# A Fourier token mixer: half of one projection moves from fp32 products to three fp32r passes, under a new table of side steps

## The chip, the core and the metric

The kernel runs on one core of one Trainium2 chip. The metric is the device time of one execution in microseconds (us): 186.82 before, the median of three runs (186.81 to 186.85). TensorE (PE) multiplies and loads its stationary weights (PEld), VectorE (DVE), ScalarE (ACT) and GpSimd (POOL) do the elementwise work, and SyncE (SP) issues most of the transfers. Each engine works through its own instructions in program order and waits on semaphores for the others.

## The reference, cut to what matters

With a depth of one, only the Fourier layer runs. It works on 512 latent tokens and, as a sequence of its own, 128 context tokens, with a width of 1024:

```python
def fourier_mix(u):                      # 4 groups of 256 channels
    ug = u.reshape(b, s, 4, 256)
    return real(fft2(ug, axes=(1, 3), norm="ortho"))   # over positions and channels

def fourier_layer(x, cond, norm_w, w_mod, b_mod, w_in, w_out):
    shift, scale, gate = split(silu(cond) @ w_mod + b_mod, 3)
    h = rms_norm(x, norm_w) * (1 + scale) + shift
    u, z = split(h @ w_in, 2)
    y = fourier_mix(u) * silu(z)
    return x + gate * (y @ w_out)
```

The outputs are the layer's result for both sequences; the two others stay empty. The results have to be close to float32.

## The kernel before

All 640 tokens are in flight together. The weights are cut into 48 pieces of 128 rows by 512 columns, and the program is a walk over 48 units n, one for each piece:

- n = 0 to 15 make z, n = 16 to 31 make u (16 to 23 the first two groups, 24 to 31 the last two), n = 32 to 47 multiply by w_out.
- Where fp32 accuracy is wanted from the faster fp32r type, an operand is split into a high half (a cast on ScalarE, `high_piece`) and a low half (the difference, mostly on VectorE, `low_piece`), and three products are added: high by high, high by low, low by high. `three` gives these pairs, and z and w_out are made so.
- u is made differently. The transform over positions is applied to the normalised input before the product with the weights (`sequence`, f16 in two halves, L575), since the product commutes with it. The input is first folded over the symmetry of the cosine and sine tables: `fold_first` to `fold_sin` make five parts c, co, so, se, ce for each quarter q of 256 channels, and `fold_split` makes f16 halves of them. `evacuate` writes the result for input chunk k, scaled by (1 + scale), as x_k. Then `product_u` (L616) multiplies x_k with the weight piece in one fp32 product per f (four to a piece, in halves of 324 and 318 columns). One fp32 product is two instructions in the profile. `fold_piece` (L210, L211) first replaces a piece's two halves by their sum and difference, which is the first step of the channel transform, and asks for piece n + 5.
- `channel` (L691 to L706) is the channel transform, in fp32r three passes, `channel_out`, `channel_last` and `alternate` assemble y, `scale_z` multiplies z by the rms factor row `rb`, `silu_z` applies SiLU, `mix` multiplies and `split_y` halves y for w_out.
- The rms factors r256 (one column per 128 tokens) are wanted along the free axis too. `spread_rms` writes them to DRAM (`rms_row`), reads them back spread over all partitions (`rt`), and `order_rms` copies them on POOL into the order of the bins.
- The conditioning: `modulate` (L296) makes the scale for chunk k on TensorE, `weigh` (L313) makes shifts and gates by a weighted sum on VectorE, one row of 1024 per condition and 128 outputs.

What runs beside the products is tied to positions in that walk: `at(n, i, step)` puts a step ahead of product i of unit n, and `run(n, i)` issues what is put there. The first eight units have their side steps written between the products (`go_ahead`, `weigh_part`). The place in the walk sets the order on every engine, and a step's transfers come into SP's queue there, too: `load_piece` waits for the buffer that its piece is to fill, and everything behind it in the queue waits with it.

Of the kernel before, what the change touches and what calls it, by code (L numbers as in the profile page):

```python
# [35 lines left out]
EVEN = np.concatenate([4 * np.arange(1, 64), 4 * np.arange(64) + 2, [0, 256]])  # L36
# [18 lines left out]
C_SEL, C_KV, C_FIRST, C_LOW, C_MISC = 0, 2, 4, 6, 7  # L55

# [56 lines left out]
def fourier_step(ctx: ExitStack, tc: tile.TileContext, a):  # L113
# [84 lines left out]

    nc.scalar.dma_start(small, a["small"])
# [34 lines left out]
    idle = const.tile([P, 512], F16, name="idle")  # L234
# [223 lines left out]
    def silu_z(e):  # L458
        for j, cols in ((1, slice(0, SL)), (0, slice(SL, T))):
            z = zs[:, e, cols]  # L460
            nc.scalar.activation(z, z, AF.Silu, bias=zs[:, e, T + j : T + j + 1])
# [6 lines left out]
    def open_folds():  # L468
# [3 lines left out]
        for n in ("ce", "se", "co", "so", "c"):  # L472
            fold[n] = [p.tile([P, D], F16, name=f"{n}_{q}") for q in "hl"]
# [10 lines left out]
    def spread_rms():  # L484

        row = dram.tile([1, 5 * P], F32, name="rms_row")
        nc.sync.dma_start(row.rearrange("o (j p) -> (o p) j", p=P), r256)
        pools["rt"] = tmp.tile([P, SL], F32, name="rt", tag="turn")
        for out, cols in ((pools["rt"], slice(0, SL)), (rb[:, SL:T], slice(SL, T))):
            nc.sync.dma_start(out, row[:, cols].to_broadcast(out.shape))  # L490

    def order_rms():
        rt = pools.pop("rt")
        for at, src in (
            (0, rt[:, 1:128:2]), (64, rt[:, 255:128:-2]),
            (128, rt[:, 4:129:4]), (160, rt[:, 252:128:-4]), (191, rt[:, 2:128:4]), (223, rt[:, 254:128:-4]),
            (255, rt[:, 0:257:256]), (257, rt[:, 385:512:2]), (321, rt[:, 383:256:-2]),
            (385, rt[:, 388:512:4]), (416, rt[:, 384:256:-4]), (448, rt[:, 386:512:4]), (480, rt[:, 382:256:-4]),
        ):
            nc.gpsimd.tensor_copy(rb[:, at : at + src.shape[-1]], src)  # L500


    fold, part = {}, {}
# [4 lines left out]
    class Parts(dict):  # L508
# [5 lines left out]
        def __missing__(self, n):  # L514
            self[n] = pools["fold"].tile([P, 256], F32, name=f"{n}_{self.q}", tag=n, bufs=1)
# [11 lines left out]
    def fold_context(q):  # L527
        c = parts_of(q)["c"] = xn[4][:, columns(q)]
        nc.scalar.activation(c, c, AF.Identity, scale=r256[:, 4:5])
# [20 lines left out]
    def fold_split(q, *names):  # L550
        for n in names:
            x = part[q][n]
# [595 lines left out]
```

## Time and profile before

| | |
|---|---|
| median of three runs | 186.82 us |
| the profiled execution | 186.77 us |
| its span | 185.0 us |
| PE busy | 179.8 us (97%), 1137 instructions |
| DVE busy | 144.5 us (78%), 318 |
| ACT busy | 88.6 us (48%), 201 |
| POOL busy | 17.5 us (9%), 57 |
| granted TensorE clock | 1.00 |

The span is the profiler's time from the first to the last instruction; 1.8 us of the execution's time lie outside it. In the views, a line names a place in the kernel printed above, `out<-in` are the program's names for the tiles, and "idle before" is how long the engine stood ahead of an instruction, with what released it. A busy engine is not the same as a limiting one: an engine counts where its work ends last.

### The profile page before, as it was taken

The numbers are of one execution on the slowest core, as the hardware profiler recorded it, in microseconds if no ns is written. First come the engines' busy times: TensorE is split into PE (matmuls) and PEld (weight loads), VectorE is DVE, ScalarE is ACT, GpSimd is POOL, SyncE is SP. The second block draws the span as 40 slices with busy tenths as digits, with TensorE's granted clock in tenths as the row PEclk, the third lists the DMA queues.
The fourth block names the chain that finished last, engine by engine and source line by source line (L and its number), as shares of the span: only waits on it lengthen the run. The fifth ranks groups of instructions, "written<-read, shape, count | busy, mean of one in ns | idle before, by whom it ended". The sixth has DMA issues, their size and how long they took to land.

```text
span 185.0 us, 3209 instructions
## 1 busy us (share of the span) xinstructions
PE 179.8 (97%) x1137; PEld 146.4 (79%) x1137; DVE 144.5 (78%) x318; ACT 88.6 (48%) x201; POOL 17.5 (9%) x57
## 2 busy tenths in 40 slices
PE   7999999999999998999999999999999999999993
PEld 2677777789999978877685786768878889999992
DVE  0444468998999999799998795589869969999422
ACT  3353733359950066977436546778774035210000
POOL 3000000000061005600002031020210000000000
PEclk9999999999999999999999999999999999999999
DMA  5999999999944007843168243120421453703532
GB/s 185 378 408 405 402 404 406 395 390 405 333 152 114 0 4 191 261 190 115 53 230 320 69 113 115 36 78 0 117 58 57 170 182 132 245 12 148 210 131 82
DMA packets 15648, 35.58 MB, mean 192 GB/s; under 512 B 2448, under 2 KB 3472, under 8 KB 15504
## 3 DMA queue, kind: packets, MB, share of 16 engines
q1 hardware_dynamic: 15488, 35.33, 53.7%
q8 instruction: 9, 0.15, 0.4%
q10 hardware_dynamic: 144, 0.04, 0.1%
q14 instruction: 7, 0.06, 0.1%
HBM read 32.75 MB, written 2.62 MB: 191 GB/s over the span
## 4 chain that ended last, share of the span: by engine, by line
PE 76%; DVE 13%; ACT 6%; DMA 2%; issue 1%; DVEq 0%
PE acc L369 25%; PE acc L616 14%; PE h L406 8%; PE s L406 8%; PE acc L379 6%; DVE junk L313 5%; PE pl L575 3%; PE pm L296 3%; DVE wl L225 3%; PE spare L280 2%; DMA ws<-in_w_in 2%; ACT zs L453 1%; PE pc L575 1%; PE acc L624 1%; ACT wh L218 1%
## 5 line engine op out<-in xcount | busy, mean ns | idle before, releaser
L616 PE MATMUL acc<-x,folded 128*128 128x324 f32 (+1 forms) x128 | 36.9, 438 | 0.0
L616 PEld LDWEIGHTS acc<-x,folded 128*128 128x128 f32 x128 | 23.5, 190 | 9.6 <-issue 1.0
L225 DVE TENSOR_TENSOR wl<-ws,wh 128x512 fp32r<-128x512 f32 x27 | 18.0, 687 | 3.0 <-ACT wh L218 2.8
L218 ACT CAST wh<-ws 128x512 fp32r<-128x512 f32 x27 | 16.3, 617 | 7.6 <-PE h L406 7.5
L313 DVE SCALAR_TENSOR_TENSOR junk<-wg,cb 128x1024 bf16<-128x1024 f32 x16 | 19.5, 1222 | 0.3
L307 DVE TENSOR_SCALAR a<-pm,b_scale,nw 128x2 f32<-128x2 f32 x8 | 2.2, 279 | 15.2 <-PE pm L306 15.1
L369 PE MATMUL acc<-yh,wh 128*128 128x512 f32 x32 | 13.0, 408 | 0.1
L369 PE MATMUL acc<-yl,wh 128*128 128x512 f32 x32 | 12.6, 394 | 0.0
L369 PE MATMUL acc<-yh,wl 128*128 128x512 f32 x32 | 12.6, 393 | 0.0
L340 ACT ACTIVATE hh<-xt,a 128x128 fp32r<-128x128 f32 (+1 forms) x15 | 7.5, 546 | 9.4 <-DVE a L307 9.4
L406 PE MATMUL h<-hl,wh 128*128 128x256 f32 (+1 forms) x40 | 11.0, 292 | 0.0
L406 PE MATMUL h<-hh,wh 128*128 128x256 f32 (+1 forms) x40 | 11.0, 292 | 0.0
L406 PE MATMUL h<-hh,wl 128*128 128x256 f32 (+1 forms) x40 | 11.0, 292 | 0.0
L406 PE MATMUL h<-yh,wh 128*128 128x256 f32 (+1 forms) x40 | 11.0, 292 | 0.0
L406 PE MATMUL h<-yl,wh 128*128 128x256 f32 (+1 forms) x40 | 11.0, 291 | 0.0
L406 PE MATMUL h<-yh,wl 128*128 128x256 f32 (+1 forms) x40 | 11.0, 290 | 0.0
L369 PE MATMUL acc<-hh,wl 128*128 128x512 f32 x32 | 10.9, 417 | 0.0
L313 DVE SCALAR_TENSOR_TENSOR junk<-folded,cb 128x1024 bf16<-128x1024 f32 x8 | 9.8, 1221 | 0.1
L313 DVE SCALAR_TENSOR_TENSOR junk<-wr,cb 128x1024 bf16<-128x1024 f32 x8 | 9.8, 1220 | 0.1
L369 PE MATMUL acc<-hh,wh 128*128 128x512 f32 x32 | 9.4, 416 | 0.1
L369 PE MATMUL acc<-hl,wh 128*128 128x512 f32 x32 | 9.3, 396 | 0.0
L347 DVE SCALAR_TENSOR_TENSOR hl<-xt,a,hh 128x512 fp32r<-128x512 f32 (+1 forms) x16 | 8.1, 548 | 1.2 <-ACT hh L340 1.2
(210 smaller groups left out, 456.1 us busy)
## 6 DMA issues: line engine op xcount, KB each, us to landing
ws<-in_w_in SPq DMA_DIRECT2D x27, 256.0 KB, 4.3
wg<-in_w_rows SPq DMA_DIRECT2D x8, 512.0 KB, 3.5
ws<-in_w_out SPq DMA_DIRECT2D x16, 256.0 KB, 2.8
wm<-in_w_scale SPq DMA_DIRECT2D x7, 512.0 KB, 8.1
xt<-in_x_t SPq DMA_DIRECT2D x8, 320.0 KB, 8.1
xn<-in_x_nat SPq DMA_DIRECT2D x5, 512.0 KB, 7.2
out<-o SPq DMA_DIRECT2D x7, 320.0 KB, 2.2
wr<-in_w_rows SPq DMA_DIRECT2D x4, 512.0 KB, 6.3
```

The lines of the kernel that those rows point to most:

```text
L218: nc.scalar.copy(hi[:, cols], raw[n][:, cols])
L225: engine.tensor_tensor(lo, t, hi, op=ALU.subtract)
L280: nc.tensor.matmul(spare[:, 0:cols], idle[:, 0:P], idle[:, 0:cols], start=True, stop=True)
L296: nc.tensor.matmul(pm[32 * j : 32 * j + 32, 0:P], cs[:, ko, :], wm[k][:, ko, :], start=ko < 4, stop=ko >= 4)
L313: nc.vector.scalar_tensor_tensor(junk, w, 1.0, cb[:, D * j : D * j + D], ALU.mult, ALU.mult, accum_out=out)
L340: nc.scalar.activation(hs[k][0][:, cols], xt[:, k, cols], AF.Identity, scale=a8[:, k, j : j + 1])
L347: nc.vector.scalar_tensor_tensor(hl[:, cols], xt[:, k, cols], a8[:, k, j : j + 1], hh[:, cols], ALU.mult, ALU.subtract)
L369: nc.tensor.matmul(chunk(n // KT)[f], w_[:, P * f : P * f + P], x_[:, 0:SL], start=first and i == 0, stop=last and i == 1,)
L379: nc.tensor.matmul(chunk(n // KT)[4], x_[:, SL:T], w_, start=first and i == 0, stop=last and i == 1)
L406: nc.tensor.matmul(half(c, f, j), w_[:, P * f : P * f + P], x_[:, tokens(c)[j]], start=first and i == 0, stop=last and i == 2,)
L575: nc.tensor.matmul(out[:, cols], fold[name][x][:, kk], t[:, at + cols.start : at + cols.stop], start=n == 0 and not add, stop=n == 2 and n ...
L616: nc.tensor.matmul(chunk(n // KT)[f][:, 0 : cols.stop - cols.start], raw[n][:, P * f : P * f + P], xs[n % KT][:, cols], start=first, stop= ...
```

## The change

`product_u` takes three fp32r passes for the pieces that have been split, which are n = 24 to 31; the first half of u stays fp32. A new step `split_x` makes the halves of x_k (a cast on ScalarE, a difference on VectorE, 642 columns), and `high_piece` and `low_piece` are called for pieces 24 to 31 as well:

```diff
+    def split_x(k):
+        tag = "al" if k < 4 else "ah"
+        xhigh[k], xlow[k] = (xpool.tile([P, X_COLS], F32R, name=f"x{q}{k}", tag=tag) for q in "hl")
+        x, hi, lo = (t[:, 0:X_END] for t in (xs[k], xhigh[k], xlow[k]))
+        nc.scalar.copy(hi, x)
+        nc.vector.tensor_tensor(lo, x, hi, op=ALU.subtract)
...
     def product_u(n, f):
...
-        nc.tensor.matmul(
-            chunk(n // KT)[f][:, 0 : cols.stop - cols.start],
-            raw[n][:, P * f : P * f + P], xs[n % KT][:, cols], start=first, stop=last,
-        )
+        k = n % KT
+        pairs = three(n, (xhigh[k], xlow[k])) if n in wsplit else ((raw[n], xs[k]),)
+        for i, (w_, x_) in enumerate(pairs):
+            nc.tensor.matmul(
+                chunk(n // KT)[f][:, 0 : cols.stop - cols.start], w_[:, P * f : P * f + P], x_[:, cols],
+                start=first and i == 0, stop=last and i == len(pairs) - 1,
+            )
```

The five folded parts of a quarter now lie side by side in one tile, so that `fold_split` covers two or three of them with one cast and one difference (512 and 768 columns, eight of each instead of twenty):

```diff
-    def fold_split(q, *names):
-        for n in names:
-            x = part[q][n]
-            hi, lo = (t[:, columns(q)] for t in fold[n])
-            nc.scalar.copy(hi, x)
-            nc.vector.tensor_tensor(lo, x, hi, op=ALU.subtract)
+    def fold_split(q, first, last):
+        x, hi, lo = (t[:, first:last, :] for t in (pools["five"], fold[0][:, q], fold[1][:, q]))
+        nc.scalar.copy(hi, x)
+        nc.vector.tensor_tensor(lo, x, hi, op=ALU.subtract)
```

The rms row is written as it lies, five numbers to a partition, and read back by one transfer that is a step of its own. `order_rms` picks the bins out of the new layout with fifteen copies (thirteen before), and in the order of the even bins number 128 moves to the end of its run:

```diff
-        row = dram.tile([1, 5 * P], F32, name="rms_row")
-        nc.sync.dma_start(row.rearrange("o (j p) -> (o p) j", p=P), r256)
-        pools["rt"] = tmp.tile([P, SL], F32, name="rt", tag="turn")
-        for out, cols in ((pools["rt"], slice(0, SL)), (rb[:, SL:T], slice(SL, T))):
-            nc.sync.dma_start(out, row[:, cols].to_broadcast(out.shape))
+        pools["row"] = dram.tile([P, 5], F32, name="rms_row")
+        nc.sync.dma_start(pools["row"], r256)
+
+    def load_rms():
+
+        pools["rt"] = tmp.tile([P, 5 * P], F32, name="rt", tag="turn")
+        row = pools["row"].rearrange("p j -> (p j)").unsqueeze(0)
+        nc.sync.dma_start(pools["rt"], row.to_broadcast([P, 5 * P]))
```

All side steps of all units stand in one table of (unit, position, step, arguments), in a new order. Two of its lines and the loop that now serves units 16 to 31:

```diff
+    (20, 0, "scale_z", 2), (20, 0, "products_mid", 0), (20, 0, "fold_split", 3, 2, 5), (20, 1, "split_x", 0),
+    (24, 1, "fold_piece", 27), (24, 1, "high_piece", 26), (24, 2, "split_mid"), (24, 2, "low_piece", 26),
...
-    for n in range(24, 32):
-        for i, f in enumerate(ORDER_V if n > 24 else range(4)):
+    for n in range(16, 32):
+        for i, f in enumerate(ORDER_U if n < 25 else ORDER_V):
             run(n, i)
             product_u(n, f)
-            if n == 31:
-                take_u(3, f)
-    for g in (2, 3):
-        shift_u(g)
+        run(n, 4)
```

In words, of the new order: the sixteen weighings of the gate all come after unit 33 (before, four came in units 20 and 21); `scale_z` for six of the eight rows comes in units 16 to 22; six of the `split_x` come in units 16 to 23 and two in units 27 and 29; `alternates` for the first two groups stands ahead of unit 27 (before, in unit 28); `modulate` 6 stands in unit 4 (before, at the start of unit 5), with the identity table and one piece more ahead of it on SP's queue; pieces 8 to 11 are fetched in the order 11, 10, 9, 8; the shifts are weighed in halves up to unit 11; SiLU on z is called by sequence; and results are written in the order 2, 3, 1, 0.

On TensorE, where z is done and the position transform starts. L432 (L538 after the change) turns the shifts, h and s are banks of z, and the rows that take c_h (fold_h after) are the first sequence. Before:

```order
L406 MATMUL h_0_552<-hh_497,wh_722 128x386
L406 MATMUL h_0_552<-hl_498,wh_722 128x386
L406 MATMUL h_0_552<-hh_497,wl_724 128x386
L432 MATMUL h_2_554<-small,shifts 128x2 x4
L575 LDWEIGHTS c_h
L575 MATMUL pc_957<-seq_h,c_h 128x130
L575 LDWEIGHTS c_l
L575 MATMUL pc_957<-seq_h,c_l 128x130
```

and now, at the same place:

```order
L512 MATMUL h_0_561<-hh_491,wh_603 128x386
L512 MATMUL h_0_561<-hl_492,wh_603 128x386
L512 MATMUL h_0_561<-hh_491,wl_677 128x386
L681 LDWEIGHTS fold_h
L681 MATMUL pc_927<-seq_h,fold_h 128x130
L681 LDWEIGHTS fold_l
```

and, at the end of that sequence:

```order
L681 MATMUL pl_928<-seq_h,fold_l 128x129
L681 LDWEIGHTS fold_h
L681 MATMUL pl_928<-seq_l,fold_h 128x129
L538 MATMUL h_2_563<-small,shifts 128x2 x4
L512 MATMUL s_2_568<-hh_352,wh_617 128x386
L512 MATMUL s_2_568<-hl_353,wh_617 128x386
```

The turn of the shifts stood ahead of the first sequence; now it stands behind it.

On SP's queue, around the rms row. ws are weight pieces, seq_h and seq_l the two halves of the position tables. Before:

```order
L189 DMA ws_599<-in_w_in 128x512
L192 DMA seq_h<-in_seq_h 128x771
L193 DMA seq_l<-in_seq_l 128x771
L189 DMA ws_626<-in_w_in 128x512
L189 DMA ws_667<-in_w_in 128x512
L189 DMA ws_671<-in_w_in 128x512
L487 DMA rms_row<-r_136 128x5x1
L490 DMA rt<-rms_row 128x512
L490 DMA rb<-rms_row 128x128
L189 DMA ws_692<-in_w_in 128x512
L189 DMA ws_726<-in_w_in 128x512
```

and now:

```order
L292 DMA ws_679<-in_w_in 128x512
L292 DMA ws_690<-in_w_in 128x512
L292 DMA ws_694<-in_w_in 128x512
L594 DMA rms_row<-r_136 128x5
L600 DMA rt<-rms_row 128x640
L292 DMA ws_768<-in_w_in 128x512
L295 DMA seq_h<-in_seq_h 128x771
L296 DMA seq_l<-in_seq_l 128x771
L292 DMA ws_876<-in_w_in 128x512
```

The tables of the position transform stood ahead of the row's write; now they stand behind the write, the read that waits for it, and one piece.

On VectorE, from the low halves of the first two groups of u to the assembly of the first outputs, during units 24 to 27. ul is a low half of u, folded<-ws is `fold_piece`, zs<-zs,rb is `scale_z`, y<-pa is `channel_out`, wl and xl are low halves of a piece and of x. Before:

```order
L675 TENSOR_TENSOR ul_1344<-u_1304,uh_1343 128x640
L210 TENSOR_TENSOR folded<-ws_1205 128x256
L211 TENSOR_TENSOR folded<-ws_1205 128x256
L456 TENSOR_TENSOR zs<-zs,rb 128x640
L210 TENSOR_TENSOR folded<-ws_1240 128x256
L211 TENSOR_TENSOR folded<-ws_1240 128x256
L727 TENSOR_TENSOR y_1373<-pa_1360,b_zero 128x257
L728 TENSOR_TENSOR y_1373<-pa_1360,b_zero 128x257
L729 TENSOR_TENSOR y_1373<-pa_1360,b_zero 128x65
L730 TENSOR_TENSOR y_1373<-pa_1360,b_zero 128x65
L456 TENSOR_TENSOR zs<-zs,rb 128x640
L210 TENSOR_TENSOR folded<-ws_1285 128x256
```

and now:

```order
L331 TENSOR_TENSOR wl_1322<-folded,wh_1312 128x512
L791 TENSOR_TENSOR ul_1325<-u_1284,uh_1324 128x640
L791 TENSOR_TENSOR ul_1340<-u_1281,uh_1339 128x640
L316 TENSOR_TENSOR folded<-ws_1193 128x256
L317 TENSOR_TENSOR folded<-ws_1193 128x256
L843 TENSOR_TENSOR y_1368<-pa_1355,b_zero 128x257
L844 TENSOR_TENSOR y_1368<-pa_1355,b_zero 128x257
L845 TENSOR_TENSOR y_1368<-pa_1355,b_zero 128x65
L846 TENSOR_TENSOR y_1368<-pa_1355,b_zero 128x65
L316 TENSOR_TENSOR folded<-ws_1202 128x256
L317 TENSOR_TENSOR folded<-ws_1202 128x256
L331 TENSOR_TENSOR wl_1390<-folded,wh_1337 128x512
```

Two scalings of z have left this stretch, and low halves of pieces have come in, the first of them ahead of the first low half of u.

More of the change, by code (lines that the diff above doesn't have):

```diff
@@ L736, in channel_out, with channel_last @@
         nc.gpsimd.tensor_copy(d1[0:1, 65:128], d1[0:1, 1:64])
-    def channel_last(g, copy=nc.vector.tensor_copy):
+    def channel_last(g):
+        copy = nc.scalar.copy if g < 2 else nc.vector.tensor_copy
         alt = pools["alts"][32 * g : 32 * g + 1, :]
@@ L785, in result, with results @@
         )
+    def results(d):
+        for j, cols in ((1, slice(0, SL)), (0, slice(SL, T))):
+            result(d, j, cols, zs[:, d, cols])
+        write(d)
     def write(d, cols=slice(0, T)):
@@ L887, in fourier_step @@
     for f in range(4):
+        run(k, 6 + f)
         product(k, f, act, (2, 1))
@@ L1068, in fourier_step @@
         run(n, 4)
-    gates()
-    for d in range(4):
-        results(d)
     for f in range(4):
         for i in range(2):
+            run(44, 2 * f + i)
             for n in range(44, 48):
```

363 lines of the change are left out of this document (165 added, 198 removed).

## The prediction

> **What bounds the kernel now.** I read the page's shares first, then each engine's busy time stage by stage, then TensorE's timeline where two stages meet.
>
> ```profile
> PE 179.8 (97%) x1137; PEld 146.4 (79%) x1137; DVE 144.5 (78%) x318; ACT 88.6 (48%) x201; POOL 17.5 (9%) x57
> PE acc L369 25%; PE acc L616 14%; PE h L406 8%; PE s L406 8%; PE acc L379 6%; DVE junk L313 5%; PE pl L575 3%; PE pm L296 3%; DVE wl L225 3%; PE spare L280 2%; DMA ws<-in_w_in 2%; ACT zs L453 1%; PE pc L575 1%; PE acc L624 1%; ACT wh L218 1%
> ```
>
> TensorE is busy 97% of the span, and most of the last chain is its products. Cutting its instructions cuts the time, but only until another engine comes too late. So the table by stage comes next (busy us of PE, PEld, DVE, ACT, POOL with instruction counts, granted clock, DMA share, GB/s):
>
> ```profile
> 12.00:42.64 30.64, 30.64 (x218) 23.37 (x218) 21.29 (x49) 15.27 (x32) 0.26 (x1) 1.00 1.03 400
> 42.64:72.70 30.06, 29.47 (x224) 27.96 (x223) 28.42 (x67) 15.79 (x36) 4.61 (x9) 1.00 0.50 161
> 72.70:101.72 29.02, 29.02 (x213) 21.58 (x211) 27.17 (x69) 18.57 (x45) 5.82 (x20) 1.00 0.58 197
> 101.72:123.60 21.88, 21.79 (x88) 15.25 (x88) 16.26 (x35) 13.37 (x36) 2.81 (x8) 1.00 0.29 87
> 123.60:153.72 30.12, 30.10 (x137) 24.23 (x138) 25.86 (x50) 17.31 (x38) 2.19 (x8) 1.00 0.30 97
> 153.72:185.00 31.28, 28.07 (x193) 27.84 (x191) 21.91 (x46) 3.35 (x6) 0.00 (x0) 1.00 0.37 135
> ```
>
> The stages are units 1 to 7, 8 to 15, 16 to 23 with the position transform, 24 to 31 with the first channel transforms, 32 to 39, and 40 to 47 with the tail. Two things stand out. VectorE is idle only 1.85 us in units 16 to 23 (29.02 - 27.17), though 5.62 in units 24 to 31. And the DMA engines are full up to 42.64 (share 1.03). TensorE has slack in hardly any stage, so a cut there counts at once.
>
> **The three passes.** The change replaces the 32 fp32 products of units 24 to 31 by three fp32r products each.
>
> ```profile
> 96.66 4.38 PE acc L616 x16
> 126.50 0.31 PE L691 MATMUL pb<-uh,ch_h 128*128 128x318 f32 x1
> ...
> 127.39 0.31 PE L706 MATMUL pa<-midl,ch_h 128*128 128x322 f32 x1
> 127.54 0.40 PE L369 MATMUL acc<-yh,wh 128*128 128x512 f32 x1
> ```
>
> Sixteen instructions of L616 are eight products (two instructions each): 4.38 / 8 = 0.55 us per product. The channel transform already runs fp32r of the same width: seven from 126.50 to 127.54, 0.149 each, so three are 0.446. That saves 0.55 - 0.446 = 0.106, and 32 times this is **3.4 us**. Below: if each of the 96 took a weight load's 190 ns (row below), 0.57 per product, 0.6 us would be lost. But the seven above load their own weights and hold 0.149.
>
> ```profile
> L616 PEld LDWEIGHTS acc<-x,folded 128*128 128x128 f32 x128 | 23.5, 190 | 9.6 <-issue 1.0
> ```
>
> The Trainium skill ("FP8 and Floating Point Precision", TensorE Precision Notes) says a true fp32 product takes four passes through the array; three would then save a quarter of 0.55, 4.4 us in all and a time near 182.4. This trace does not quite agree: 0.55 / 0.149 is 3.7 passes, and the measured pair decides.
>
> **Two gaps of TensorE that go.** Ahead of the position transform the shifts' turn (L432) waits for ScalarE:
>
> ```profile
> 70.54 0.34 PE L406 MATMUL h<-hl,wh 128*128 128x386 f32 x1
> 70.72 0.33 PE L406 MATMUL h<-hh,wl 128*128 128x386 f32 x1
> 71.64 1.05 PE L432 MATMUL h<-small,shifts 128*128 128x2 f32 x8 [0.59 <-ACT zs L453]
> 72.56 0.22 PE L575 MATMUL pc<-seq_h,c_h 128*128 128x130 f16 x1
> ```
>
> Neighbours of that width are 0.18 apart, so the next start could have been 70.90; it came at 71.64, 0.74 lost, and the eight short ones held TensorE 0.92 more. With the turn behind the first sequence the 0.74 goes, and some of the 0.92 may; I take **1.0** (0.7 to 1.4).
>
> ```profile
> 121.71 0.63 PE L369 MATMUL acc<-yh,wh 128*128 128x512 f32 x1
> 122.19 0.39 PE L369 MATMUL acc<-yh,wl 128*128 128x512 f32 x1
> 122.42 0.40 PE L369 MATMUL acc<-yl,wh 128*128 128x512 f32 x1
> ...
> 123.11 0.40 PE L379 MATMUL acc<-wh,yl 128*128 128x512 f32 x1
> 123.62 0.50 PE L369 MATMUL acc<-yh,wh 128*128 128x512 f32 x1
> ```
>
> At unit 32 the steps 0.48 and 0.51 stand where neighbours take 0.23: 0.53 lost, the second part because VectorE copies u late, behind a mixing step. In the new order that copy is asked for after unit 31's products, with VectorE's queue shorter there. I take **0.5** (0 to 0.6).
>
> **What VectorE and ScalarE get.** Each of the eight x needs a cast and a subtraction, 642 wide, and each of the eight pieces a cast and a subtraction, 512 wide.
>
> ```profile
> L755 DVE TENSOR_TENSOR yl<-y,yh 128x640 fp32r<-128x640 f32 x8 | 6.4, 820 | 1.2 <-ACT yh L754 1.2
> L225 DVE TENSOR_TENSOR wl<-ws,wh 128x512 fp32r<-128x512 f32 x27 | 18.0, 687 | 3.0 <-ACT wh L218 2.8 <-issue 0.2
> L754 ACT CAST yh<-y 128x640 fp32r<-128x640 f32 x8 | 5.7, 722 | 2.2 <-DVE y L749 2.1
> L218 ACT CAST wh<-ws 128x512 fp32r<-128x512 f32 x27 | 16.3, 617 | 7.6 <-PE h L406 7.5
> L555 DVE TENSOR_TENSOR so_l<-so,so_h 128x256 f16<-128x256 f32 x4 | 1.7, 420 | 0.1
> L313 DVE SCALAR_TENSOR_TENSOR junk<-wg,cb 128x1024 bf16<-128x1024 f32 x16 | 19.5, 1222 | 0.3
> 119.82 0.82 DVE L755 TENSOR_TENSOR yl<-y,yh 128x640 fp32r<-128x640 f32 x1
> 120.56 0.82 DVE L749 TENSOR_TENSOR y<-y,zs 128x640 f32<-128x640 f32 x1
> ```
>
> Successive instructions overlap by 0.08 (119.82 to 120.56 is 0.74 for 0.82), so VectorE pays 0.74 per x and about 0.60 per piece: 8 x 1.34 = 10.7 us. ScalarE pays at most 8 x (0.72 + 0.62) = 10.7, and with 18.57 of 29.02 and 13.37 of 21.88 busy it has room. On VectorE these go by stage:
> - Units 16 to 23: six x and two pieces, +5.6. Four scalings of z (640 wide, 0.74) come here from later, +3.0. Four weighings of the gate leave, at 1.22 and a read of the sum, about 1.26 each: -5.0. Twelve or so of the twenty 256-wide splits merge into wider ones: on the line through 420 ns at 256 and 820 at 640, eight merged ones cost 6.6 against 8.4 for all, some -1.1 here. Net +2.5: 27.17 becomes 29.7, in a stage that stays 29.0 long: **more than full**, and the rest must find room in the idle time of the stages on both sides (1.64 before it, 30.06 - 28.42).
> - Units 24 to 31: two x and six pieces, +5.1; three scalings, two mixings, one piece and one split leave, -5.0. About 16.3 again, but the stage now lasts 21.9 - 3.4 - 0.5 = 18.0. Idle falls from 5.6 to 1.7.
> - From unit 32: the four weighings arrive, +5.0 on 25.86 + 21.91 in 61.4 us. Room enough, and the gates are wanted only near the end.
>
> The other steps that change place (shift weighings taken in halves, squares, SiLU in two parts, pieces 8 to 11 fetched in reverse, two copies more on POOL, which is busy 5.82 of 29.02) stay on engines or queues with room in their stage, behind products of TensorE. I price them at nothing; what cover they lack is in the next charge.
>
> So VectorE covers its new work only if it hardly ever waits. Following the queues in order with these durations, I find it late by 0.3 at the first channel transform (the low half of u, behind the low half of piece 26), by about 0.4 at the alternating sums ahead of unit 27 (there ScalarE's copies of the first bank), and just in time for piece 28; unit 32 has about 1.3 to spare. Each hand-over that I put too low falls on these. I charge **-1.2** (0.7 to 2.5).
>
> **The rms row and the tables behind it.** The row now goes out as 128 runs of five numbers, not 640 single ones. The tables of the position transform are loaded behind the row's write, its read and one piece on SP's queue; before they went ahead of all that.
>
> ```profile
> 56.82 0.38 SPq L487 DMA_DIRECT2D rms_row<-r  x1
> 68.00 0.33 SPq L490 DMA_DIRECT2D rt<-rms_row  x1
> SPq L490 <- DMA rms_row<-r: 10.7, 1, 10.7
> 60.00:68.00 8.00, 1.00 0.03 2
> DMA to landing us min/median/max: 3.6/4.1/4.6
> DMA to landing us min/median/max: 4.4/4.4/4.4
> ```
>
> The write held SP 10.7 us; the second last line is the row's reads, the last the first table. No row shows the new write. It costs between 3.6 (a small transfer at its quickest) and 10.7. From 60 to 68 us SP issued nothing and the DMA engines moved 2 GB/s (fourth line), so the 10.7 is not bytes; I take it as going with the number of pieces, 10.7 / 5 and a fixed part, about 4 to 5. Issued near 57.8 (three quarters of a unit later), it lands by 63, the tables are issued by 64 to 66 and land by 70.4, wanted at 70.7. **Nothing**, with little to spare. The Trainium skill ("DMA: Bandwidth & Descriptors", Specifications) says pieces under 512 bytes cost a read and a write each; twenty bytes stay under that, so by it only the count improves, as I reckon.
>
> **The first 42 us.** Scale 6 is used earlier in unit 4 instead of at the start of unit 5.
>
> ```profile
> wm<-in_w_scale SPq DMA_DIRECT2D x7, 512.0 KB, 8.1
> 20.11 0.33 SPq L158 DMA_DIRECT2D wm<-in_w_scale  x1
> 29.89 0.64 PE L296 MATMUL pm<-wm,cs 128*32 128x128 f32 x16
> ```
>
> It landed near 28.2 (20.11 + 8.1) for 29.89. Its products now stand about 1.5 earlier, at 28.4, and a table and a piece (64 and 256 KB, 0.33 MB) more lie ahead of it, 0.8 us at 400 GB/s: 29.0. **-0.3** (0 to -0.6, to -1.5 if others slip too).
>
> **Sum.** 3.4 + 1.0 + 0.5 - 1.2 - 0.3 = 3.4. The profiled execution took 186.77 (span 185.0), within 0.05 of the 186.82 median; 186.77 - 3.4 = **183.4**. With the ends of the terms, 181.6 to 184.8.
>
> **Rivals.**
> *VectorE sets the pace of units 16 to 31 (slower).* Its work there becomes 29.7 + 16.3 = 46.0. If it still idles 7.5 us, as before (1.85 + 5.62), because each step waits for a product, an evacuation or a cast, the two stages last 53.5 instead of 50.9; less the 1.0 of the gap this is +1.6: **188.4**. It is slower than before once 6.3 or more of the 7.5 stay, and half way (4.5) gives 185.4. For it: both stages are full. Against: much of the old idle time is waiting for fp32 products, which get shorter, and the casts are put well ahead.
> *The write stays slow.* 10.7 from 57.8 is 68.5; then the read, a piece and the tables are issued, the second near 69.9, landing 74.4: TensorE stands 3.7 ahead of the first sequence. VectorE catches up meanwhile, so 183.4 + 3.7 - 1.2 = **185.9**. It decides from a write of about 7 us on. Against: the count of pieces falls fivefold. The Trainium skill ("TensorE: Matmul & The Clock Gate", What's actually happening) says the array drops to half clock after an idle window of about 3.4 us; then up to 3.4 us more would run at half speed, 1.7 us, near 187.6. No row here shows it, the clock stands at 1.00 in every stage and TensorE never idles that long.
> *Three passes are no cheaper*, held by weight loads: +0.6 for the -3.4, 187.4 with all else. Against: the 0.149 above.
>
> **How the numbers follow.** Forecast 0.62. VectorE half way (184.8 to 186.4) 0.15, all the way 0.09. Slow write 0.09, a fifth of it with the lower clock. No cheaper passes 0.03, anything else 0.02. Within 0.2% of 186.82 (186.45 to 187.19) is no change that can be told. Faster: 0.62 + 0.15 + most of the slow write, 0.83. Same 0.07, from the edges of the slow write and of VectorE's case. Slower 0.10. The likeliest alone is 181.6 to 184.8; the range reaches up to 186.4.
>
> **What would show it.** Right: products of unit 24 on 0.446 us apart; the first sequence near 70.7 with no ScalarE wait ahead; SP's wait for the row 4 to 5; VectorE over 95% busy in units 16 to 31; unit 32 near 118. Wrong: an idle TensorE over 1 us for a low half in units 24 to 31, waits for seq_h, or waits for scale 6.

## The result

The changed kernel takes 184.5 us, the median of four runs (184.05 to 184.96); the kernel before took 186.83 beside it. The ratio is 0.9872, with a 95% interval from 0.9846 to 0.9898: 2.3 us faster, where 3.4 were forecast (183.4, range 181.6 to 186.4). A second measurement gave 184.26 (184.2 to 184.38) against 187.19, ratio 0.9832 (0.9804 to 0.986).

The profiled execution of the changed kernel is the quickest of the four, 184.05 with a span of 182.2, 2.8 less than before. Its busy time by stage (units 16 to 23 from the first sequence on; 24 to 31; 32 to 39; the rest), with the columns of the table before. That table ends its stage of units 24 to 31 six products into unit 32 (123.60; unit 32 starts at 121.71), so the lengths of the second and the third stage can't be compared with it directly:

```profile
70.96:101.66 30.70, 30.51 (x222) 22.66 (x221) 29.71 (x62) 22.40 (x42) 3.63 (x9) 1.00 0.35 109
101.66:119.10 17.44, 17.36 (x116) 16.44 (x114) 16.07 (x36) 15.76 (x41) 3.68 (x6) 1.00 0.32 93
119.10:150.74 31.64, 31.64 (x145) 25.19 (x143) 29.96 (x57) 18.37 (x39) 6.32 (x10) 1.00 0.37 118
150.74:182.20 31.46, 28.42 (x193) 28.21 (x191) 24.46 (x50) 4.03 (x8) 0.00 (x0) 0.99 0.47 166
```

VectorE works 29.71 and 16.07 us in units 16 to 31, 95% of the two stages. The prediction had 29.7 and 16.3, the second up to the place six products into unit 32; up to there (120.48) VectorE now works 17.45 us.

Where the 2.8 us came from is read from where TensorE's instructions start. First, the place where z is done and the position transform starts:

```profile
70.78 0.34 PE L512 MATMUL h<-hh,wl 128*128 128x386 f32 x1
70.96 0.23 PE L681 MATMUL pc<-seq_h,fold_h 128*128 128x130 f16 x1
71.93 0.22 PE L538 MATMUL h<-small,shifts 128*128 128x2 f32 x1
72.80 0.42 PE L512 MATMUL s<-hh,wh 128*128 128x386 f32 x1
```

The first sequence follows the last product of z without a gap. Its start is 1.60 earlier than before, and the turn of the shifts takes 0.87 of that afterwards.

Then the three passes, and the two places in their neighbourhood where TensorE loses time:

```profile
101.42 0.55 PE L732 MATMUL acc<-xh,wh 128*128 128x324 f32 x1
101.81 0.31 PE L732 MATMUL acc<-xl,wh 128*128 128x324 f32 x1
...
109.07 0.31 PE L732 MATMUL acc<-xh,wl 128*128 128x324 f32 x1
109.46 0.74 PE L831 MATMUL pb<-u,ch 128*32 128x322 f32 x4
110.12 0.42 PE L732 MATMUL acc<-xh,wh 128*128 128x324 f32 x1
...
119.10 0.39 PE L475 MATMUL acc<-yh,wh 128*128 128x512 f32 x1
```

From 110.12 to 119.10 stand 20 products in 8.98 us, 0.449 each, the first step of 0.26 among them; without its 0.11 over the usual 0.15 they take 0.444 each. The alternating sums at 109.46 come 0.24 late: 0.39 after their neighbour instead of 0.15 (where nothing waits, at 110.96 in the version with three moves below, that step takes 0.24).

Two more losses. In unit 23 the first product waits for x 7, whose evacuation ScalarE reaches late (first TensorE, then ScalarE, then VectorE):

```profile
97.66 0.70 PE L732 MATMUL acc<-x,folded 128*128 128x318 f32 x2
98.55 1.86 PE L732 MATMUL acc<-x,folded 128*128 128x324 f32 x6 [0.19 <-issue]
96.83 0.62 ACT L324 CAST wh<-folded 128x512 fp32r<-128x512 f32 x1 [1.14 <-DVE folded L317]
97.36 0.36 ACT L723 ACTIVATE x<-pc,a 128x130 f32<-128x130 f32 x1
93.84 2.29 DVE L719 TENSOR_TENSOR xl<-x,xh 128x642 fp32r<-128x642 f32 x3
96.39 0.42 DVE L317 TENSOR_TENSOR folded<-ws 128x256 f32<-128x256 f32 x1
```

ScalarE has the cast of piece 25 ahead of the evacuation. The cast waits 1.14 us for VectorE's fold of that piece, which stands behind three low halves of x. The profile gives the product's wait no releaser ("issue"); that it is the evacuation is borne out by the versions below that put the evacuation ahead of the cast, in whose profiles the wait is gone. And in unit 32 the alternating sums of the last two groups (next rows, then POOL) hold TensorE from 122.64 to 123.78, 1.14 us, where they took 0.67 before:

```profile
122.31 0.40 PE L475 MATMUL acc<-yl,wh 128*128 128x512 f32 x1
122.64 1.21 PE L831 MATMUL pe<-u,ch 128*32 128x322 f32 x4
123.78 0.50 PE L475 MATMUL acc<-yh,wh 128*128 128x512 f32 x1
120.55 2.25 POOL L784 TENSOR_TENSOR u<-u,small 128x2 f32<-128x2 f32 x1
```

The sums read u behind its shift (`shift_u`), two steps on POOL that touch two columns. The first of them for the last group takes 2.25 us here, and the second ends at 123.06, in the middle of the sums.

The rms row's new write holds SP for 1.1 us, not 10.7 and not the 4 to 5 that were reckoned, and the tables are issued seven microseconds before they are wanted:

```profile
SPq L600 <- DMA rms_row<-r: 1.1, 1, 1.1
58.01 0.33 SPq L594 DMA_DIRECT2D rms_row<-r  x1
59.48 0.33 SPq L600 DMA_DIRECT2D rt<-rms_row  x1
63.67 0.43 SPq L295 DMA_DIRECT2D seq_h<-in_seq_h  x1
28.78 0.65 PE L402 MATMUL pm<-wm,cs 128*32 128x128 f32 x16 [0.28 <-DMA wm<-in_w_scale]
```

The last row is the wait for scale 6, 0.28 us, as long as was charged.

### The profile page after: what moved, and what is told of

It reads as the page before. It is cut to its first block, busy times and chain, and to the rows that moved or that the text cites. A ratio compares the mean times of both kernels' runs of the same rounds, so it can differ in the third digit from the quotient of the medians.

```text
span 182.2 us, 3274 instructions
## 1 busy us (share of the span) xinstructions
PE 177.2 (97%) x1169; PEld 148.7 (82%) x1169; DVE 152.9 (84%) x322; ACT 97.2 (53%) x205; POOL 25.3 (14%) x59
## 4 chain that ended last, share of the span: by engine, by line
PE 78%; DMA 15%; DVE 2%; POOL 1%; issue 1%; ACT 0%; SPq 0%
PE acc L475 18%; PE h L512 17%; PE acc L732 15%; PE s L512 14%; DMA wr<-in_w_rows 5%; PE acc L485 4%; DMA wm<-in_w_scale 4%; DMA xt<-in_x_t 4%; PE pl L681 4%; DMA small<-in_small 2%; POOL y L850 1%; PE h L530 1%; DVE ul L791 1%; PE pc L681 1%; PE acc L740 1%
## 5 line engine op out<-in xcount | busy, mean ns | idle before, releaser
L732 PE MATMUL acc<-x,folded 128*128 128x324 f32 (+1 forms) x64 | 19.1, 441 | 0.2 <-issue 0.2
L732 PEld LDWEIGHTS acc<-x,folded 128*128 128x128 f32 x64 | 11.6, 190 | 5.6 <-issue 1.7
L732 PE MATMUL acc<-xh,wh 128*128 128x324 f32 (+1 forms) x32 | 10.3, 320 | 0.0
L475 PE MATMUL acc<-hh,wl 128*128 128x512 f32 x32 | 10.1, 408 | 0.0
L732 PE MATMUL acc<-xh,wl 128*128 128x324 f32 (+1 forms) x32 | 9.9, 310 | 0.0
L732 PE MATMUL acc<-xl,wh 128*128 128x324 f32 (+1 forms) x32 | 9.9, 310 | 0.0
```

The lines of the kernel that those rows point to most:

```text
L475: nc.tensor.matmul(chunk(n // KT)[f], w_[:, P * f : P * f + P], x_[:, 0:SL], start=first and i == 0, stop=last and i == 1,)
L732: nc.tensor.matmul(chunk(n // KT)[f][:, 0 : cols.stop - cols.start], w_[:, P * f : P * f + P], x_[:, cols], start=first and i == 0, stop=l ...
```

## The experiments

Each kernel was timed beside the kernel before on the same chip. The twelve kernels were spread over three chips, on which the kernel before had medians of 187.07, 187.15 and 187.19.

### The second half of u in fp32 again

```diff
-    (24, 1, "high_piece", 26), (24, 2, "low_piece", 26), ... (and all others of 24 to 31)
-    (16, 4, "split_x", 1), (20, 1, "split_x", 0), ... (all eight)
-    (25, 3, "fold_piece", 29),
+    (26, 0, "fold_piece", 29),
```

> The changed kernel with units 24 to 31 in fp32 again: no halves of x, no halves of pieces 24 to 31; everything else, the new order too, stays (the fold of piece 29 moves half a unit later, since its buffer is read longer). Theory A (three passes save 0.10 per product, 3.3 us in all, and about 1.1 of it is given back by steps that wait for a loaded VectorE and ScalarE): 186.4 to 186.9, with the waits at units 23 and 27 gone. Theory B (the waits are a matter of the new order alone and stay): 187.5 to 187.9. Theory C (the passes save much less than their spacing says): 185.0 to 185.8.

Measured: 186.05 (185.56 to 187.34), ratio 0.9937 (0.9907 to 0.9967); between theory C's range and theory A's, in neither. The passes are worth 1.6 to 1.8 us net (beside 184.26 and 184.5), not the 3.3 that TensorE saves in them; the new order without them is worth about 1.0 (186.05 for 187.07). What the profile shows is theory A's mechanism, a gain of TensorE of which VectorE's added work takes a part back, with a larger part than A gave it. In the stage table of this kernel (units 16 to 23, then 24 to 31):

```profile
71.23:101.24 30.01, 30.01 (x221) 22.73 (x221) 24.77 (x54) 17.77 (x34) 3.27 (x9) 1.00 0.36 107
101.24:121.50 20.26, 20.26 (x84) 14.30 (x83) 12.69 (x31) 11.58 (x33) 1.48 (x6) 1.00 0.27 86
```

VectorE has 4.9 and 3.4 us less to do, and TensorE is busy throughout. From the first sequence to the last product of unit 23, with its sum over the middle rows ahead, it needs 29.46 us where the changed kernel needs 30.06 (70.96 to 101.02): 0.6 of the loss there comes with the passes' work on VectorE and ScalarE. The alternating sums behind unit 32 take 0.67 here and 1.14 in the changed kernel, another 0.47. With the 0.35 of unit 27 (below) that is 1.4 of the 3.3.

The shift ahead of those sums is quick here:

```profile
122.67 0.20 POOL L784 TENSOR_TENSOR u<-u,small 128x2 f32<-128x2 f32 x1
```

VectorE is idle from 121.75 to 122.95 in this kernel. In the changed one it runs three subtractions without a gap from 120.59 to 122.75, and POOL's step, begun at 120.55, ends at 122.80. In all eleven profiles of kernels with the passes and the new order the step takes 2.24 or 2.25 us. So the late sums come with the passes, through POOL; that VectorE's run is what holds POOL is suggested by these times, but was not tested.

### The rms row in single numbers again

```diff
-        nc.sync.dma_start(pools["row"], r256)
+        nc.sync.dma_start(pools["row"].rearrange("o (j p) -> (o p) j", p=P), r256)
```

> The changed kernel with the rms row written as before, 640 single numbers, and read back in one transfer; the order of steps stays. Theory A (the write takes as long as it has pieces): SP waits about 10 us for it, the position tables land near 74, TensorE stands 3 to 4 us ahead of the first sequence; 186.0 to 188.0, the upper half if the clock drops after the wait. Theory B (the write was slow for another reason than its pieces, or the tables have more room than reckoned): 184.3 to 185.0.

Measured: 191.45 (190.88 to 193.47), ratio 1.0218 (1.0166 to 1.027), 7 us above the changed kernel. Theory A's mechanism with a larger price; the columns of the stretches are those of the stage table:

```profile
SPq L599 <- DMA rms_row<-r: 10.5, 1, 10.5
74.77 0.22 PE L680 MATMUL pc<-seq_h,fold_h 128*128 128x130 f16 x1 [3.41 <-DMA seq_h<-in_seq_h]
74.77:76.00 1.23, 1.08 (x10) 0.95 (x11) 0.00 (x0) 0.37 (x1) 1.23 (x8) 0.63 0.40 152
76.00:81.00 5.00, 5.00 (x30) 4.52 (x29) 2.32 (x7) 1.19 (x2) 0.83 (x3) 0.50 0.08 22
81.00:82.00 1.00, 1.00 (x7) 0.99 (x6) 1.00 (x3) 0.36 (x1) 0.00 (x0) 0.54 0.42 154
82.00:83.00 1.00, 1.00 (x8) 1.00 (x7) 0.37 (x1) 0.97 (x4) 0.21 (x2) 1.00 0.00 0
```

The first sequence starts 3.81 later (74.77 for 70.96), which the prediction had as 3.7. The granted clock (the column behind POOL's) is 0.50 from 76 to 81 and has a mean of 0.63 over the 1.23 us ahead of that and of 0.54 over the one behind. If the clock had only the values 1.00 and 0.50, that is half clock from about 75.1 to 81.9, 6.8 us. At half clock these lose 3.4 us, and the work from the first sequence to the first product of u takes 8.51 us (74.77 to 83.28) instead of 5.08 (70.96 to 76.04): another 3.4. The two make 7.2 of the span's 7.1.

### The same, with the tables ahead of the row

```diff
-    (12, 3, "load_tables"),
+    (8, 3, "load_tables"),
```

> The changed kernel with the rms row written as 640 single numbers, and the position tables loaded in unit 8, ahead of that write on SP's queue, as the kernel before does. Theory A (the slow write hurts only because the tables stand behind it): SP still waits 10 us for the row, TensorE doesn't wait ahead of the first sequence, and the time is within 0.7 of the changed kernel, 184.1 to 185.2. Theory B (the late rms row itself holds VectorE, whose first scaling of z stands in unit 16 behind POOL's copies): 186 to 188, with VectorE waiting 2 us or more for the row.

Measured: 186.06 (185.62 to 186.31), ratio 0.993 (0.9905 to 0.9955), 1.6 to 1.8 above the changed kernel: the time is at the lower edge of theory B's range, but B's sign, a wait of VectorE of 2 us or more for the row, is not there. VectorE waits 1.2, and the longest of the waits of TensorE that the changed kernel doesn't have is one for POOL:

```profile
PE acc L731 <- POOL x L711: 0.5, 1, 0.5
PE pl L680 <- DVE fold_l L670: 0.4, 1, 0.4
POOL rb L614 <- DMA rt<-rms_row: 14.4, 1, 14.4
DVE zs L562 <- POOL rb L614: 1.2, 1, 1.2
```

POOL waits for the late row, and behind its copies stands its next work, the shift columns of the x (L711), which TensorE wants for its first product of u. VectorE waits 1.2 for `rb` and is late with a folded part. So the wide write is worth about 1.7 us in this order even where no table stands behind it. TensorE's two waits are 0.9 of that; the rest was not traced to a step.

### The passes alone, in the old order

```diff
+    for n in range(26, 32):
+        at(n - 1, 1, high_piece, n)
+        at(n - 1, 2, low_piece, n)
+    for n, k in ((24, 3), (25, 4), (26, 5), (27, 6), (28, 7)):
+        at(n, 3, split_x, k)
```

and the first three `split_x` in units 20 to 22, pieces 24 and 25 in 22 and 23.

> The kernel before with nothing but the three passes in units 24 to 31, the halves of x and of pieces 24 to 31 put into its own order one unit ahead of their use or more. Theory A (VectorE is nearly full in units 16 to 31, and with the gate's weighings still there and 10.7 us more it sets the pace): the 3.3 us saved on TensorE are mostly eaten, 185.5 to 188.0, with TensorE waits of more than 1 us for low halves. Theory B (the old idle time of VectorE, 7.5 us in these units, takes the new work): 183.5 to 184.5.

Measured: 198.85 (198.09 to 199.74), ratio 1.0621 (1.0575 to 1.0666): 11.7 slower than before, far above either range. TensorE waits for casts and low halves, here summed and then at the longest; then the stage from unit 24:

```profile
PE acc L626 <- DVE wl L225: 4.6, 5, 2.4
PE acc L626 <- ACT wh L218: 4.5, 3, 2.0
130.41 0.47 PE L626 MATMUL acc<-xh,wl 128*128 128x324 f32 x1 [2.44 <-DVE wl L225]
103.00:135.00 32.00, 22.91 (x116) 19.57 (x115) 24.71 (x49) 19.72 (x48) 5.73 (x11) 0.89 0.22 66
```

VectorE is busy 24.71 of 32.00 us there, so its load alone does not explain the waits. It waits for casts, ScalarE waits for folds and for products, and TensorE for both. The clock falls to 0.89 in the mean of the stage. Another placing of the same steps in the old order was not tried, so this is one bad order, not the price of the old one.

### Four weighings of the gate back in units 20 and 21

```diff
-    (33, 0, "weigh_gate", 0, 0), (36, 4, "weigh_gate", 0, 1), (36, 4, "weigh_gate", 1, 0), (37, 2, "weigh_gate", 1, 1),
+    (20, 3, "weigh_gate", 0, 0), (20, 3, "weigh_gate", 0, 1), (21, 3, "weigh_gate", 1, 0), (21, 3, "weigh_gate", 1, 1),
```

> The changed kernel with the four weighings of the gate of the first two rows in units 20 and 21 again, as before the change: 5.0 us of VectorE work put back into units 16 to 24. Theory A (VectorE is full from unit 16 to 28, idle under 2 us there): 3 to 5 us longer, 187.5 to 189.5, TensorE waits for low halves in units 21 to 28. Theory B (there is room left; the waits of the changed kernel are a matter of order): 184.4 to 185.5.

Measured: 192.08 (191.07 to 192.17), ratio 1.0244 (1.0211 to 1.0277), 7.8 above the changed kernel on the same chip. Theory A, and past its range; not with the waits for low halves that it names, but with a single wait for an evacuation. (The loads of the two gate rows move with the weighings, to the start of unit 16.) TensorE, ScalarE, and the stretch in which the wait ends:

```profile
103.66 3.56 PE L732 MATMUL acc<-x,folded 128*128 128x324 f32 x6 [5.02 <-issue]
101.95 0.62 ACT L324 CAST wh<-folded 128x512 fp32r<-128x512 f32 x1 [4.05 <-DVE folded L317]
102.48 0.36 ACT L723 ACTIVATE x<-pc,a 128x130 f32<-128x130 f32 x1
101.70:106.00 4.30, 2.34 (x5) 1.56 (x6) 3.56 (x7) 3.08 (x6) 0.30 (x2) 0.50 0.62 201
106.00:108.00 2.00, 2.00 (x11) 0.49 (x9) 1.24 (x4) 0.68 (x2) 0.48 (x3) 0.60 0.21 71
```

Of the 5.0 us put back, nearly all come out as a single wait of 5.02 at unit 23 (0.19 without them), through the same three queues as above: the fold is late, the cast waits, the evacuation stands behind the cast. The clock is at 0.50 by the end of that wait and has a mean of 0.60 from 106 to 108, so it is back at about 107.6: 3.9 us of work at half clock, 2.0 lost. 4.8 more of waiting and 2.0 make the 6.8 by which the span is longer than the changed kernel's on that chip (189.3 for 182.5).

### The turn of the shifts ahead of the first sequence again

```diff
-    (14, 3, "sequence", 0), ... (14, 3, "turn_shifts"),
+    (14, 3, "turn_shifts"), (14, 3, "sequence", 0),
```

> The changed kernel with the turn of the shifts ahead of the first sequence again. Theory A (the gap ahead of the turn is ScalarE's copy of z and the shifts, and comes back): the first sequence starts 1.6 later, and the time grows by 0.7 to 0.8 against the changed kernel. Theory B (the shifts are ready by then, as ScalarE's queue is in another order): no gap, the time within 0.2 of the changed kernel.

Measured: 184.66 (184.5 to 185.74), ratio 0.9868 (0.9834 to 0.9902), 0.4 above the changed kernel's 184.26 on that chip, with intervals that overlap. It lies between the theories in time, and its profile is theory B's:

```profile
71.08 0.34 PE L512 MATMUL h<-hh,wl 128*128 128x386 f32 x1
71.26 0.95 PE L538 MATMUL h<-small,shifts 128*128 128x2 f32 x8
72.06 0.22 PE L681 MATMUL pc<-seq_h,fold_h 128*128 128x130 f16 x1
```

The turn follows at once. The gap of 0.74 went because ScalarE copies the shifts and z earlier, not because the turn stands elsewhere. In the kernel before it copies both shifts (from 69.39 on) and five parts of z behind the casts of the first folded parts, and the turn starts at 71.64, as the last of these copies ends; here the shifts come five microseconds earlier, and the last part of z is copied by 69.80:

```profile
71.18 0.41 ACT L453 COPY zs<-h 128x256 f32<-128x256 f32 x1
...
64.18 0.37 ACT L533 COPY shifts<-h 128x256 f32<-128x256 f32 x1 [4.70 <-PE h L530]
69.32 0.48 ACT L559 COPY zs<-s 128x386 f32<-128x386 f32 x1 [0.96 <-PE s L512]
```

(one row of the kernel before, then two of this one). In the two profiles from that chip the difference is 0.2 (184.5 for 184.28).

### Scale 6 back in unit 5

```diff
-    (4, 10, "modulate", 6),
+    (5, 0, "modulate", 6),
```

> The changed kernel with one step moved: the products of scale 6 stand at the start of unit 5 again, as before the change. Theory A (the early use of scale 6 waits for its transfer, 0.28 us in the profile, and more in the slower of the four runs, 184.05 to 184.96): no wait for scale 6 in the profile, median 183.9 to 184.2, the runs closer together than 0.4. Theory B (the spread and the wait come from somewhere else in the first 42 us or later): median 184.3 to 184.6, and a spread of about 0.9 as in the changed kernel.

Measured: 184.33 (183.83 to 185.1), ratio 0.9825 (0.9782 to 0.9868), the changed kernel's time. No wait for scale 6 is left in the profile, and no gain is to be seen: theory B's time. The runs still differ by 1.3 us, so scale 6 does not make their spread. Part of the spread has another place. The profiled execution is the slowest of the six, 185.1, and TensorE's first product of unit 0 waits in it (TensorE, then ScalarE):

```profile
8.42 1.20 PE L475 MATMUL acc<-hh,wh 128*128 128x512 f32 x4 [0.98 <-ACT wh L324]
7.96 0.75 ACT L324 CAST wh<-zs 128x256 fp32r<-128x256 f32 x2 [1.97 <-DMA zs<-in_w_in]
```

ScalarE's cast of the very first weight piece stands 1.97 us for the piece's transfer. In the changed kernel's profile the same cast starts at 6.54 and the product at 7.02, without a wait of TensorE. Up to there the two programs are the same, so this is a difference between executions: when the first piece lands.

### Four moves, three moves, and two that build on them

```diff
-    (23, 0, "high_piece", 25), (23, 0, "evacuate", 7),
+    (23, 0, "evacuate", 7), (23, 0, "high_piece", 25),
-    (27, 0, "alternates", 0, 1), ... (28, 0, "channel_last", 0),
+    (28, 0, "alternates", 0, 1), (28, 2, "channel_last", 0),
-    (32, 4, "alternates", 2, 3),
+    (34, 0, "alternates", 2, 3),
```

With scale 6 in unit 5:

> The changed kernel with four steps moved: scale 6 back to unit 5, the evacuation of x 7 ahead of the cast of piece 25, the alternating sums of the first two groups to unit 28 and those of the last two to unit 34. Theory A (each of these waits is paid by TensorE on its own: 0.3, 0.4, 0.35 and 0.47 us): 183.0 to 183.4, and none of the four waits in the profile. Theory B (VectorE and ScalarE set the pace there, and a wait that is taken away returns at the next step that needs them): 183.9 to 184.4, with new waits in units 24 to 33.

Measured: 183.34 (182.83 to 184.27), ratio 0.9781 (0.9737 to 0.9825): theory A's range. Its profiled execution, 184.09, is again a slow one of its six, with the same wait of 1.11 at 8.34, the first product of unit 0.

The three moves without scale 6:

> The changed kernel with three steps moved and scale 6 left where the change has it: the evacuation of x 7 ahead of the cast of piece 25, the alternating sums of the first groups to unit 28, of the last to unit 34. Theory A (the wait of 1.1 us for the cast of piece 6 that came with scale 6 in unit 5 cost the version with four moves just that): 182.2 to 182.6, no wait of TensorE over 0.3 us after the first 5 us. Theory B (work moved later loads ScalarE and VectorE elsewhere, so that the four moves together are as good as it gets): 183.2 to 183.6.

Measured: 183.61 (183.27 to 184.56), ratio 0.9819 (0.9779 to 0.9859): theory B's time. The expectation speaks of a wait of 1.1 us that came with scale 6, for the cast of piece 6. That was misread from a row that names no time: it is the wait at the first product, above, which does not hang on scale 6. In the profile of this version the three waits that the moves aim at are gone. Its first sequence starts at 71.50 though, 0.54 later than in the profile of the changed kernel, after waits of 0.3 each for scale 6 and for two results of ScalarE in the first 42 us, in code that it shares with the changed kernel, whose profile has scale 6's wait and 0.2 for one of the two.

With piece 6 and the identity table behind scale 6 in the queue, besides:

> The version with three moves, and the transfers of piece 6 and of the identity table behind that of scale 6 on SP's queue, instead of ahead of it. Theory A (scale 6 waits for its transfer because 320 KB lie ahead of it): the 0.28 us wait of the changed kernel is gone, 0.2 to 0.4 faster than the version with three moves. Theory B (the transfer is late for another reason, or piece 6 becomes the late one): no gain, or a new wait for the cast of piece 6.

Measured: 183.34 (182.84 to 184.56), ratio 0.9797 (0.9762 to 0.9832). No wait for scale 6 is left; 0.27 less than the version with three moves, within both spreads.

And with the last low halves of the folded parts ahead of one scaling of z:

```diff
-    (20, 0, "scale_z", 2), (20, 0, "products_mid", 0), (20, 0, "fold_split", 3, 2, 5),
+    (20, 0, "products_mid", 0), (20, 0, "fold_split", 3, 2, 5), (20, 0, "scale_z", 2),
```

> The version with three moves and the two transfers behind scale 6, and besides the last low halves of the folded parts ahead of one scaling of z on VectorE's queue. Theory A (each wait of TensorE is worth its own length): 0.17 us less than without the last step, 183.0 to 183.4, about 1.2 below the changed kernel, with no wait at the seventh sequence. Theory B (VectorE is full there, and the wait moves on to a later low half): 183.3 to 183.8, with a new wait in units 21 to 25.

Measured: 183.89 (183.2 to 184.84), ratio 0.9815 (0.9782 to 0.9848), beside 184.26 for the changed kernel unaltered:

> The changed kernel itself, unaltered, beside the other three on one chip, as their measure: 184.0 to 185.0, 2.0 to 2.9 below the kernel before.

The wait at the seventh sequence went, and this one came, at the first channel transform:

```profile
PE pb L809 <- DVE ul L791: 0.5, 1, 0.5
```

That is theory B's mechanism: VectorE is full there, and what one step gains the next one waits. The four versions with moves have medians 0.4 to 0.9 below the changed kernel's 184.26, but three of them ran on other chips than it, and their intervals all overlap with the one of that measurement (0.9804 to 0.986). They may be better; it is not shown, nor which is best.

## Why the prediction came out as it did

The direction, the range and most terms held; the gain was 2.3 instead of 3.4 (2.8 in the profiled spans). Term by term, with the profiled starts:

- **Three passes, 3.4.** Right. Before, the 14 products from the alternating sums to unit 32 took 7.42 us, and the first step of what follows 0.25 more than its neighbours: 0.548 each. Now it is 0.444. 32 times the difference is 3.3. The four-pass rule of the Trainium skill ("FP8 and Floating Point Precision", TensorE Precision Notes) would have made it 4.4; the measurement bears out the 3.7 passes of the rows.
- **The gap ahead of the transform, 1.0.** Measured 0.8 (1.66 between the last product of z and the first sequence before; 0.87 for the turn now). Its cause was put in the wrong place: with the turn ahead of the sequence again there is no gap either.
- **Unit 32, 0.5.** This is the step that failed, and it came to nothing: units 32 to 39 need 31.64 now; before, from 121.96 (where unit 32 would have started without its first 0.25) to 153.56, they needed 31.60. Of the 0.53, only the second part was a wait. It went: 0.28, and 0.11 on the step behind it. The first part, 0.25 at 121.71, is no stall but belongs to the fp32 products ahead of it. With fp32 products in the new order it is still there (121.30 to 121.77), while the second is gone; and the runs of nine, five and fourteen fp32 products before the change take 4.72, 2.45 and 7.42 us, which makes 0.54 to 0.55 for each product only with the 0.25 that the step behind each run is longer. So it was in the 3.4 already, and was counted twice. And the alternating sums of the last groups, which now stand just behind unit 32, took 0.47 back. The prediction asked for the copy of u only, not for the next step, which needs u's shift, and has no term for that shift on POOL: its first step took 2.25 us, where it takes 0.20 without the passes.
- **VectorE, -1.2.** Measured -1.3. Units 16 to 23 lost 0.7 (from the first sequence to unit 24, without the turn: 29.83 now, 29.09 before), of it 0.43 at x 7 and 0.17 at a folded part. Unit 27 lost 0.35, where 0.4 was forecast; 0.15 of it was waiting, and the other 0.20 is left where nothing waits, in the version with three moves. The first channel transform lost 0.17, where 0.3 was forecast. Of VectorE's two loads the first was right, 29.71 for 29.7; the second, cut as the prediction cut it, was 17.45 for 16.3. The place was only half right: the largest of these waits was not for a low half, but for an evacuation behind a cast on ScalarE that a late fold of VectorE held.
- **Scale 6, -0.3.** The wait was 0.28, of which 0.07 is left at unit 8 (42.71 for 42.64).
- **The rms row, nothing.** Right for the tables. The write itself was reckoned at 4 to 5 us and held SP for 1.1.
- **The rest.** Units 40 to 47 and the tail took the same, 31.46 from unit 40 on for 31.44 before. So 3.3 + 0.8 - 1.3 - 0.1 leaves 2.7 of the 2.8. The median lies 0.45 above the profiled execution, and runs of one kernel differ by up to 2.3 us (186.49 to 188.82, the kernel before on one chip). One place where that arises is shown, the landing of the first weight piece before 9 us, worth about 1 us in two profiles; what else makes it was not found, and moving scale 6 did not change it.

The likeliest range was added up wrongly. The ends of the terms as stated give 182.1 to 185.8 (186.7 with scale 6 at its worst), not 181.6 to 184.8. The measured 184.5 lies in both.

The rivals. *VectorE sets the pace* did not happen, but was not far: with four weighings more in the same stage the kernel takes 192.08. That is not the case that was priced at 188.4, as VectorE has 5.0 us more to do in it. The reckoning spread the delay over the idle time; in the queues of that kernel it arrived as one wait and brought the clock down. *The write stays slow* was priced at 185.9, or 187.6 with the lower clock by the Trainium skill ("TensorE: Matmul & The Clock Gate", What's actually happening). With the slow write it took 191.45: the wait was right (3.81 for 3.7), but the half clock cost 3.4, not 1.7, as it lasted for nearly two of the windows of 3.4 us that the Trainium skill gives there, not one. And the wide write was given no worth but that for the tables; it is worth about 1.7 even where no table stands behind it, in part since POOL's copies hold POOL's own next work. *No cheaper passes* is out.

## What to carry to other kernels

Where engines work in order, the cost of added work is not its share of a busy time but the first instruction that it makes late: look in every queue for what stands behind the instruction that will wait, and do this for the engine between the two as well (here ScalarE, whose cast for one step held the evacuation for another). When a nearly full engine gets more work, take as much away from the same stage: the same passes were worth 1.7 us with the weighings moved out, and with them back the kernel was 7.8 us slower. Look for transfers that are cut into many tiny pieces, and price whatever is queued behind them with them. And the shortest step on a fourth engine has to be followed, too: POOL's shift of two columns had no term in the sum and held TensorE for 0.47 us.

## What the runs showed of the hardware that was not expected

- After a wait of TensorE of 3.41 us the granted clock stood at 0.50 from about 75.1 to 81.9, 6.8 us, and cost about as much again as the wait. In the kernel with the old order the clock was reduced after shorter waits that followed each other closely: 0.54 and 0.61 in the mean of 110 to 112 and 112 to 114, after waits of 2.03 (to 107.78) and 1.05 (to 109.40); 0.66 and 0.50 from 130 to 134, after one of 2.44 that followed others of 0.5 to 1.7 us. The wait of 5.02 us in the kernel with the weighings back took it to 0.50 too, before the wait was over, until about 107.6. Single waits up to 1.1 us left it at 1.00.
- A write of 640 pieces of 4 bytes to DRAM held its reader for 10.3 to 11.2 us in each of the four kernels that had it, and one of 128 pieces of 20 bytes, the same 2,560 bytes, for 1.1. That is less than in proportion to the pieces. Their number and their size changed together, so it is not shown which of the two counts.
- TensorE's step from an fp32 product to an fp32r one took 0.39 us where its neighbours take 0.15 (101.42 to 101.81), as did the steps behind each run of fp32 products before. The runs ahead of them are shorter by 0.15 to 0.29 than 0.548 for each product makes, so such a step is to be read together with the run, and not as a stall.
- A step of POOL on two columns took 2.25 us while VectorE ran subtractions without a gap, and a copy of 63 columns 1.97 (107.46 to 109.43, with VectorE at work without a gap from 106.38 to 109.33). Both end within 0.1 us of VectorE's run. With VectorE idle the first took 0.20. The reason was not tested.
